# Scatter marks on one engine, attention products over the whole array, and six more steps before a transpose

## The chip, the core and the metric

The kernel runs on one core of one Trainium2 chip. The core has five engines with queues of their own: PE (TensorE, matrix products; its weight loads are listed as PEld), DVE (VectorE), ACT (ScalarE), POOL (GpSimd) and SP, which issues most transfers. Each queue runs in the order in which it was laid out; between queues, instructions wait on semaphores. The metric is the device time of one execution in microseconds.

## The reference

A network of three blocks on 512 tokens of width 1024, batch 1, all in float32:

```python
def reference(x, ...):
    x = first_block(x, ...)        # hybrid mixer (recurrence and pooling), then expert layer
    return second_block(x, ...)    # even mixer, conv FFN, odd mixer, conv FFN

def peer_ffn(h, wq, keys, u_tab, v_tab):             # the expert layer, 16384 experts
    q = (xb @ wq).reshape(T, 8, 2, 128)
    s = einsum('thpc,hpnc->thpn', q, keys)           # two key halves, 128 scores each
    v1, i1 = top_k(s[:, :, 0], 16); v2, i2 = top_k(s[:, :, 1], 16)
    sc, pos = top_k(v1[..., :, None] + v2[..., None, :], 16)   # over 256 candidates
    idx, gate = take_along_axis(i1 * 128 + i2, pos), softmax(sc)
    act = gelu(einsum('td,thkd->thk', xb, u_tab[idx]))
    return einsum('thk,thkd->td', gate * act, v_tab[idx])

# even mixer: MLA attention (8 heads, values of 64) and difference attention (4 heads, two maps of 64 rows)
# odd mixer: dilated attention (3 groups of 4 heads of 64, one joint softmax) and
#            stick-breaking attention (4 heads of 64); both causal, blocks of 128 queries
```

## The kernel before

A float32 weight tile of 1024 columns is loaded, rounded by ACT into a high part (L64) and split by DVE or POOL into a low part (L67); three products per pair (`mm3`, L117 to L119) replace one in full precision. `K.unit` does load, cast and split. Where no engine is named for the split, POOL and DVE take turns.

The program is traced by Python generators and then laid out: for each engine the planner orders the instructions by the moment at which its own model has them ready, with program order as priority, so the queues don't follow the program line by line. `interleave(main, n_main, fill, n_fill)` mixes two generators step by step: after step i of `main`, `fill` has made i * n_fill / n_main steps.

**Expert layer.** The first 128 tokens ("gathered" tokens) fetch their experts' rows one by one with indirect transfers of POOL (`chosen`, L621). For the other 384 tokens the layer is computed densely: for each of 128 expert tiles `up` makes 24 products of 384 columns (tile `pu`), the result is multiplied by a gate and `down` adds it into `pacc`. The gates come from `scatter` (L483): in 24 groups of 16 tokens, each with 4 steps of 4 tokens, one-hot marks are formed and multiplied: `gu` (L498, 128 elements per partition) and `lw` (L500, 256) mark the two parts of an index, `gu` is multiplied by the gate (L502), `e[1]` marks the other half (L507, 512 elements) and `e[0]` is the product of `gu` and `lw` (L511). `e[0]` is shared out: POOL makes four tokens' worth in the even steps and three in the odd ones, where DVE makes the fourth. PE multiplies `e[0]` by `e[1]` (L517), 8 instructions a step, ACT copies the gates out (L520, L521), and SP sends most of them to memory (`pe_gd`).

While search and scatter run, `ahead` computes the first `EARLY` expert tiles: `FIRST` steps after each of seven heads of the search, the rest interleaved with `scatter`. The dense stage then starts with `EARLY` tiles that need no `up`, two steps of `chosen` beside each, and goes on with 118 - `EARLY` tiles interleaved with the rest of `chosen` and then `end`. `end` (L725) squares the gathered tile on ACT, yields once, and then normalises, transposes on PE (`pf`) and evicts it.

**Attention.** `Attn.scores` makes one product per segment (`sp`, L785), `transposed` turns the probabilities (`tp`, L805), and the values follow (`po`). The products run in float32, each as two instructions of PE. MLA scores use 96 rows. MLA values (L999) take 64 columns of the array per head, two heads sharing a bank. Difference scores, dilated scores (tiles `od_qk`) and stick scores (L1114) use 64 rows of a tile that holds two heads; dilated values (L1191) and stick values (L1142) 64 columns. In the odd block, `proj` copies each projected tile out of PSUM on ACT, and `out` turns a finished pair of heads into a high and a low part. The projections that are still missing fill the steps of the attention.

Of the kernel before, what the change touches and what calls it, by code (L numbers as in the profile page):

```python
# [13 lines left out]
F32 = mybir.dt.float32  # L14
# [9 lines left out]
S = 512  # L24
# [310 lines left out]
EARLY = 25  # L335
# [64 lines left out]
class Peer:  # L400
# [84 lines left out]
    def scatter(self, wk, ps, slots, pool, iota):  # L485
# [6 lines left out]
        own = 0, 1, 0, 1  # L492
        for t16 in range(NB):
            ts = slice(16 * t16, 16 * t16 + 16)
            g = wk.tile([128, 16, 8], F32, name=k.name("gu"), tag="gu")
            lw = wk.tile([128, 16, 16], BF16, name=k.name("lw"), tag="lw")
# [5 lines left out]
            (V if t16 else G).tensor_tensor(out=g, in0=g, in1=slots[:, 0, ts].unsqueeze(2).to_broadcast([128, 16, 8]), op=ALU.mult)  # L502
            for q in range(4):
# [5 lines left out]
                for eng, lo, hi in ((G, 0, 4 - own[q]), (V, 4 - own[q], 4)):  # L509
                    if lo < hi:  # L510
                        eng.tensor_tensor(out=e[0][:, lo:hi].rearrange("p t (u l) -> p t u l", u=8),  # L511
                                          in0=g[:, 4 * q + lo:4 * q + hi].unsqueeze(3).to_broadcast([128, hi - lo, 8, 16]),
                                          in1=lw[:, 4 * q + lo:4 * q + hi].unsqueeze(2).to_broadcast([128, hi - lo, 8, 16]),
                                          op=ALU.mult)
# [130 lines left out]
    def run(self, x, free_x, dram, ctx2, pre, ps, tag):  # L645
# [9 lines left out]
        with ExitStack() as ctx, ExitStack() as gctx, ExitStack() as ectx:  # L655
# [57 lines left out]
            with open_pool(tc, name="pe_gc", bufs=2) as self.gpool:  # L713
                interleave(dense, 118 - EARLY, chained(fill, self.end(st, 0, acc, g, gpre, tail, ps)), 252)
# [10 lines left out]
    def end(self, st, t, u, g, gpre, pool, ps):  # L725
# [13 lines left out]
        yield  # L739
# [100 lines left out]
def finished(k, st, gen, gpost, gpre, pool):  # L840

    for done in gen:
# [7 lines left out]
        yield  # L850

# [5 lines left out]
def even(k, st, a, pre):  # L857
# [3 lines left out]
    with ExitStack() as ctx:  # L861
# [26 lines left out]
        with open_pool(tc, name="ev_lr", bufs=1) as lr, open_pool(tc, name="ev_wk", bufs=2) as wk:  # L888
# [96 lines left out]
            def mla(h, i):  # L985
# [10 lines left out]
                if j not in po:  # L996
                    po[j] = st.bank("po")
                for b in range(i + 1):
                    T.matmul(po[j][z * 64:z * 64 + 64, q], vm[:, b, h * 64:(h + 1) * 64], pT[b],  # L999
                             start=b == 0, stop=b == i)  # L1000
                if z == 1 and i == NT - 1:
                    p = po.pop(j)
                    A.copy(ohi[j], p)
                    V.tensor_tensor(out=olo[j], in0=p, in1=ohi[j], op=ALU.subtract)
# [14 lines left out]
        def diff(h, i):  # L1019
# [3 lines left out]
            for z in range(2):  # L1023
                rows = slice(64 * z, 64 * z + 64)
                ss.append(at.scores([(dq[h][rows, q], dk[h][rows, 0:n], n, 0.125, bias[:, h, 512 - n:])],
                                    512, "s" if z else "s2"))
# [27 lines left out]
def odd(k, st, a, pre):  # L1054
# [3 lines left out]
    with ExitStack() as ctx:  # L1058
# [7 lines left out]
        qk = [tile(f"od_qk{i}") for i in range(12)]  # L1066
# [24 lines left out]
        def out(j, p, q=slice(0, S)):  # L1091
            A.copy(ohi[j][:, q], p)
            V.tensor_tensor(out=olo[j][:, q], in0=p, in1=ohi[j][:, q], op=ALU.subtract)

        with open_pool(tc, name="od_st", bufs=2) as wk:
# [4 lines left out]
            sq = [wk.tile([128, S], F32, name=f"od_s{i}", bufs=1) for i in range(4)]  # L1100
            po = {}

            def stick(h):

                z, j = h % 2, h // 2
                rows = slice(64 * z, 64 * z + 64)
                q, kt = sq[j], sq[2 + j]
# [3 lines left out]
                for kb in (3, 2, 1, 0):  # L1111
                    n = 512 - 128 * kb
                    zp = st.bank("sp")
                    T.matmul(zp[:, :n], kt[rows, kb * 128:(kb + 1) * 128], q[rows, kb * 128:], start=True, stop=True)  # L1114
# [22 lines left out]
                if j not in po:  # L1137
                    po[j] = st.bank("po")
                p = po[j]
                for kb in range(4):  # L1140
                    n = 512 - 128 * kb
                    T.matmul(p[rows, kb * 128:], vt[:, kb, 768 + h * 64:768 + (h + 1) * 64],  # L1142
                             at_[:, off[kb]:off[kb] + n], start=kb == 0, stop=kb == 3)
                yield
                if z == 1:
                    out(j, po.pop(j))
# [989 lines left out]
```

## Time and profile before

| | us |
|---|---|
| three runs | 3182.52, 3187.62, 3186.67 (median 3186.67) |
| profiled execution | 3186.87, its span 3185.1 |
| busy in the span: PE, PEld | 3011.8 (95%), 2505.0 (79%) |
| busy: DVE, ACT, POOL | 2045.6 (64%), 1344.0 (42%), 1021.9 (32%) |
| chain that ended last | PE 68%, DVE 7%, the rest 1% and less each |

The stages in this execution: mixer to about 500 us, search of the expert layer to 699, scatter to 873, dense experts to 1858, even block to some 2115, FFN to some 2515, odd block to some 2820, FFN to the end. Busy shares are means over stages with different limits, so the table by stage is what to read first. PE's matmuls overlap: one instruction's duration holds its latency, and the distance from one start to the next is what it costs in a stream. The same is true, by some 0.08 us, of DVE.

### The profile page before, as it was taken

Reading aid. Unit: us, or ns where it says so; the run is one execution under the profiler, and the core shown is the slowest. Engines: PE = TensorE matmul, PEld = TensorE weight load, DVE = VectorE, ACT = ScalarE, POOL = GpSimd, SP = SyncE. Lnnn points to the kernel's source line nnn. Section 1 sums busy time; section 2 is a strip of 40 time slices with the busy share of each in tenths; the row PEclk is TensorE's granted clock in tenths of the full one; section 3 lists DMA queues with packets and bytes.
Section 4 is the critical chain, followed back from the end, with each engine's and each line's share of the span. In section 5 each row is a group of like instructions: output and inputs, shape, how many; then the busy total and the mean of one; then the engine's idle time right before and its main releaser. Section 6 shows DMA issues by size and latency. Waiting matters only on the chain.

```text
span 3185.1 us, 45861 instructions
## 1 busy us (share of the span) xinstructions
PE 3011.8 (95%) x17602; PEld 2505.0 (79%) x17602; DVE 2045.6 (64%) x3762; ACT 1344.0 (42%) x2448; POOL 1021.9 (32%) x754
## 2 busy tenths in 40 slices
PE   7888999998799999999999999989999999999999
PEld 5656668988678998999998986668888776688887
DVE  5777747999987888888888445565551333554522
ACT  5333344346633333333334355564442354444422
POOL 4322234667612444444443021222222221122221
PEclk9878999999999999999999999999999999999999
DMA  2000134333346999999998432323233242123332
GB/s 89 24 16 20 39 121 162 94 110 149 131 137 215 344 335 329 330 334 338 334 336 289 126 116 67 112 73 108 93 99 93 87 133 83 51 88 100 93 99 80
DMA packets 176203, 476.09 MB, mean 149 GB/s; under 512 B 18768, under 2 KB 68688, under 8 KB 175728
## 3 DMA queue, kind: packets, MB, share of 16 engines
q1 hardware_dynamic: 139120, 338.93, 32.2%
q0 software_dynamic: 36864, 134.23, 11.8%
q8 instruction: 138, 2.26, 0.3%
q14 instruction: 81, 0.66, 0.1%
HBM read 448.59 MB, written 24.51 MB: 149 GB/s over the span
## 4 chain that ended last, share of the span: by engine, by line
PE 68%; DVE 7%; issue 1%; ACT 1%; DMA 1%; POOL 0%; DVEq 0%; ACTq 0%; POOLq 0%
PE pacc L119 6%; PE pacc L117 5%; PE pacc L118 5%; PE up L117 5%; PE up L118 5%; PE up L119 5%; PE pu L117 5%; PE pu L119 5%; PE pu L118 5%; PE acc L117 3%; PE acc L119 3%; PE acc L118 3%; DVE e L507 2%; PE pj L117 2%; PE pj L118 2%; PE pj L119 2%
## 5 line engine op out<-in xcount | busy, mean ns | idle before, releaser
L64 ACT CAST whi<-raw 128x1024 fp32r<-128x1024 f32 x494 | 518.1, 1051 | 685.3 <-PE pu L118 173.8
L67 DVE TENSOR_TENSOR wlo<-raw,whi 128x1024 fp32r<-128x1024 f32 x359 | 454.5, 1267 | 446.6 <-ACT whi L64 444.6
L67 POOL TENSOR_TENSOR wlo<-raw,whi 128x1024 fp32r<-128x1024 f32 x135 | 328.7, 2436 | 1109.9 <-ACT whi L64 1040.7
L117 PE MATMUL pu<-pe_hhi,whi 128*128 128x384 f32 x1024 | 350.5, 342 | 6.2 <-ACT whi L64 3.7
L119 PE MATMUL pu<-pe_hhi,wlo 128*128 128x384 f32 x1024 | 348.6, 340 | 0.2 <-DVE wlo L67 0.2
L118 PE MATMUL pu<-pe_hlo,whi 128*128 128x384 f32 x1024 | 348.1, 340 | 0.0
L118 PE MATMUL pacc<-wlo,ahi 128*128 128x512 f32 x768 | 304.1, 396 | 0.0
L117 PE MATMUL pacc<-whi,ahi 128*128 128x512 f32 x768 | 296.2, 396 | 3.1 <-ACT ahi L592 3.1
L119 PE MATMUL pacc<-whi,alo 128*128 128x512 f32 x768 | 292.2, 398 | 3.4 <-DVE alo L593 3.4
L119 PE MATMUL up<-res_h,wlo 128*128 128x512 f32 (+1 forms) x752 | 283.2, 377 | 1.0 <-DVE wlo L67 1.0
L117 PE MATMUL up<-res_h,whi 128*128 128x512 f32 (+1 forms) x752 | 283.8, 378 | 0.0
L118 PE MATMUL up<-res_h,whi 128*128 128x512 f32 (+1 forms) x752 | 283.5, 377 | 0.0
L621 POOL DMA_INDIRECT row<-pe_v,pe_gs x128 | 160.4, 1253 | 217.6 <-DVE pe_acc L637 208.5
L621 POOL DMA_INDIRECT row<-pe_rows,pe_gs x128 | 163.9, 1281 | 185.5 <-DVE pe_gs L628 165.7
L253 DVE SCALAR_TENSOR_TENSOR u<-up,ffn_par,u 128x511 f32<-128x511 f32 (+1 forms) x176 | 131.4, 748 | 142.7 <-ACT u L251 139.6
L117 PEld LDWEIGHTS pu<-pe_hhi,whi 128*128 128x128 f32 x1024 | 193.9, 189 | 11.6 <-ACT whi L64 4.2
L118 PEld LDWEIGHTS pu<-pe_hlo,whi 128*128 128x128 f32 x1024 | 194.0, 189 | 4.3
L119 PEld LDWEIGHTS pu<-pe_hhi,wlo 128*128 128x128 f32 x1024 | 193.6, 189 | 1.1 <-DVE wlo L67 0.8
L119 PEld LDWEIGHTS pacc<-whi,alo 128*128 128x128 f32 x768 | 144.9, 189 | 38.2 <-DVE alo L593 3.8
L117 PEld LDWEIGHTS pacc<-whi,ahi 128*128 128x128 f32 x768 | 144.7, 189 | 33.2 <-ACT ahi L592 3.8
L118 PEld LDWEIGHTS pacc<-wlo,ahi 128*128 128x128 f32 x768 | 144.8, 188 | 31.0
L637 DVE SCALAR_TENSOR_TENSOR pe_acc<-row,pe_gs,pe_acc 128x1024 f32<-128x1024 f32 x128 | 163.7, 1279 | 5.9 <-DMA row<-pe_v,pe_gs 5.5
(499 smaller groups left out, 6557.3 us busy)
## 6 DMA issues: line engine op xcount, KB each, us to landing
raw<-pe_u SPq DMA_DIRECT2D x128, 512.0 KB, 5.9
raw<-pe_v SPq DMA_DIRECT2D x128, 512.0 KB, 6.1
raw<-ffn_up SPq DMA_DIRECT2D x88, 512.0 KB, 3.5
raw<-ffn_dn SPq DMA_DIRECT2D x44, 512.0 KB, 3.6
pe_gd<-go SPq DMA_DIRECT2D x24, 784.0 KB, 3.3
gc<-pe_gd SPq DMA_DIRECT2D x12, 1536.0 KB, 15.5
mraw<-mx_in SPq DMA_DIRECT2D x80, 128.0 KB, 2.2
raw<-pe_wq SPq DMA_DIRECT2D x16, 512.0 KB, 3.8
```

Source lines behind the costliest of these rows:

```text
L64: nc.scalar.copy(hi, raw)
L67: eng.tensor_tensor(out=lo, in0=raw, in1=hi, op=ALU.subtract)
L117: mm(out, l[0], r[0], start=first, stop=False)
L118: mm(out, l[0], r[1], start=False, stop=False)
L119: return mm(out, l[1], r[0], start=False, stop=last)
L253: V.scalar_tensor_tensor(out=u[:, d:], in0=p[:, :S - d], scalar=par[:, o + 2 - d:o + 3 - d], in1=u[:, d:], op0=ALU.mult, op1=ALU.add)
L507: V.tensor_tensor(out=e[1], in0=slots[:, 3, o:o + 4].unsqueeze(2).to_broadcast([128, 4, 128]), in1=iota.unsqueeze(1).to_broadcast([128, 4, ...
L621: G.indirect_dma_start(out=r, out_offset=None, in_=table[z], in_offset=bass.IndirectOffsetOnAxis(ap=idx[:, j:j + 1], axis=0))
L637: V.scalar_tensor_tensor(out=acc, in0=row("v", j), scalar=w[:, j:j + 1], in1=acc, op0=ALU.mult, op1=ALU.add)
```

## The change

It has three parts. In `scatter` all products `e[0]` and the first `gu` product go to DVE, `gu` and `lw` move from the pool `wk` to the pool of `go`, `EARLY` is 26 instead of 25, and the splits of the early expert tiles from number 11 on are all given to DVE. In the attention, MLA, dilated and stick products use 128 rows and columns: queries are kept once per head with zeros in the other head's 64 rows (`apart`, `blank`), values multiply the columns of both heads, and each head has a bank (or, for the last dilated heads, half of one) of which its own 64 rows are evicted. In `end`, the gathered tile yields seven times between squares and transposes, and the filler's count is 258 instead of 252.

```diff
-EARLY = 25
+EARLY = 26
@@ scatter
-        own = 0, 1, 0, 1
-            g = wk.tile([128, 16, 8], F32, name=k.name("gu"), tag="gu")
-            lw = wk.tile([128, 16, 16], BF16, name=k.name("lw"), tag="lw")
+            g = pool.tile([128, 16, 8], F32, name=k.name("gu"), tag="gu")
+            lw = pool.tile([128, 16, 16], BF16, name=k.name("lw"), tag="lw")
-            (V if t16 else G).tensor_tensor(out=g, in0=g, in1=slots[:, 0, ts]...)
+            V.tensor_tensor(out=g, in0=g, in1=slots[:, 0, ts]...)
-                for eng, lo, hi in ((G, 0, 4 - own[q]), (V, 4 - own[q], 4)):
-                    if lo < hi:
-                        eng.tensor_tensor(out=e[0][:, lo:hi]..., op=ALU.mult)
+                V.tensor_tensor(out=e[0].rearrange("p t (u l) -> p t u l", u=8),
+                                in0=g[:, 4 * q:4 * q + 4]..., in1=lw[:, 4 * q:4 * q + 4]..., op=ALU.mult)
@@ ahead
-            early.append((yield from self.up(pool, ps, hhi, hlo, i, f"early{i}")))
+            eng = self.k.nc.vector if UP * i >= 7 * FIRST else None
+            early.append((yield from self.up(pool, ps, hhi, hlo, i, f"early{i}", eng)))
@@ run
-                interleave(dense, 118 - EARLY, chained(fill, self.end(st, 0, acc, g, gpre, tail, ps)), 252)
+                interleave(dense, 118 - EARLY, chained(fill, self.end(st, 0, acc, g, gpre, tail, ps)), 258)
@@ end
-        yield
+        for _ in range(1 + 6 * (t == 0)):
+            yield
@@ new
+HALF = (slice(0, 64), slice(64, 128))
+def apart(k, dst, src):
+    k.nc.scalar.copy(dst[0][HALF[0]], src[HALF[0]])
+    k.nc.vector.tensor_copy(dst[1][HALF[1]], src[HALF[1]])
+def blank(k, pairs):
+    for z in range(2):
+        for pair in pairs:
+            k.nc.gpsimd.memset(pair[z][HALF[1 - z]], 0.0)
@@ mla
-                if j not in po:
-                    po[j] = st.bank("po")
+                if i == 0:
+                    po[h] = st.bank("po")
-                    T.matmul(po[j][z * 64:z * 64 + 64, q], vm[:, b, h * 64:(h + 1) * 64], pT[b], ...)
-                if z == 1 and i == NT - 1:
-                    p = po.pop(j)
-                    A.copy(ohi[j], p)
+                    T.matmul(po[h][:, q], vm[:, b, j * 128:(j + 1) * 128], pT[b], ...)
+                if i == NT - 1:
+                    p = po.pop(h)[HALF[z]]
+                    A.copy(ohi[j][HALF[z]], p)
@@ odd
-        qk = [tile(f"od_qk{i}") for i in range(12)]
+        pool = (fctx.enter_context(open_pool(tc, name="od_j0", bufs=1, side="right")), big)
+        qs = [[tile(f"od_q{i}{z}", pool=pool[i % 2]) for z in range(2)] for i in range(6)]
+        ks = [tile(f"od_k{i}", pool=pool[i % 2]) for i in range(6)]
+        blank(k, qs)
-                A.copy(qk[f], st.project1(k.unit(a["od_in"][f]), "pj"))
+                p = st.project1(k.unit(a["od_in"][f]), "pj")
+                if f < 6:
+                    apart(k, qs[f], p)
+                else:
+                    A.copy(ks[f - 6], p)
-        def out(j, p, q=slice(0, S)):
+        def out(h, p, q=slice(0, S)):
+            j, r = h // 2, HALF[h % 2]
+            A.copy(ohi[j][r, q], p[r])
-            sq = [wk.tile([128, S], F32, name=f"od_s{i}", bufs=1) for i in range(4)]
+            sq, sk = (qs[1], qs[3]), (ks[1], ks[3])
@@ stick
-                    T.matmul(zp[:, :n], kt[rows, kb * 128:(kb + 1) * 128], q[rows, kb * 128:], ...)
+                    T.matmul(zp[:, :n], kt[:, kb * 128:(kb + 1) * 128], q[:, kb * 128:], ...)
-                    T.matmul(p[rows, kb * 128:], vt[:, kb, 768 + h * 64:768 + (h + 1) * 64], ...)
+                    T.matmul(p[:, kb * 128:], vt[:, kb, 768 + j * 128:896 + j * 128], ...)
@@ dilated
-                segs.append((qk[f][rows, q], qk[6 + f][rows, lo * 128:n], w, 0.125, ...))
+                segs.append((qs[f][z][:, q], ks[f][:, lo * 128:n], w, 0.125, ...))
-            p = po[key][rows, 0:128] if j else po[key][rows, q]
+            p = po[key][:, z * 128:z * 128 + 128] if j else po[key][:, q]
-                T.matmul(p, vt[:, kb, hd * 64:(hd + 1) * 64], pT[b], ...)
+                T.matmul(p, vt[:, kb, f * 128:(f + 1) * 128], pT[b], ...)
+        fctx.close()
```

## Rows read from the trace of the kernel before

**Rows 1.** Busy us by stretch: PE, PEld, DVE, ACT, POOL (instructions), clock, DMA share, GB/s.
```profile
500.00:699.00 199.00, 185.62 (x1349) 182.70 (x1348) 178.84 (x709) 79.01 (x164) 117.16 (x78) 0.99 0.34 110
699.00:873.00 174.00, 138.12 (x947) 127.28 (x945) 168.31 (x221) 113.42 (x401) 120.33 (x100) 0.96 0.35 134
1030.00:1858.00 828.00, 826.40 (x4113) 746.92 (x4113) 637.73 (x789) 301.29 (x420) 319.53 (x256) 1.00 0.87 305
1938.00:2046.00 108.00, 105.11 (x537) 76.60 (x536) 52.09 (x133) 55.11 (x122) 19.33 (x8) 1.00 0.26 83
2556.00:2685.00 129.00, 129.00 (x535) 92.88 (x534) 49.69 (x94) 66.85 (x122) 29.66 (x13) 1.00 0.36 112
2685.00:2800.00 115.00, 113.99 (x594) 78.16 (x593) 55.14 (x174) 51.13 (x101) 12.50 (x8) 1.00 0.16 49
```

**Rows 2.** Timeline of DVE in the scatter stage, POOL silent until 737.76: start, us, instruction.
```profile
736.64 0.41 DVE L500 TENSOR_TENSOR lw<-pe_slots,pe_iota 128x256 bf16<-128x256 f32 x1
736.98 0.68 DVE L507 TENSOR_TENSOR e<-pe_slots,pe_iota 128x512 f32<-128x512 f32 x1
737.58 0.28 DVE L511 TENSOR_TENSOR e<-gu,lw 128x128 f32<-128x128 f32 x1
737.78 0.28 DVE L502 TENSOR_TENSOR gu<-gu,pe_slots 128x128 f32<-128x128 f32 x1
```

**Rows 3.** Timeline of POOL and DVE in the scatter stage, later.
```profile
840.68 1.13 POOL L511 TENSOR_TENSOR e<-gu,lw 128x512 f32<-128x512 f32 x1 [0.53 <-PE gp L517]
840.83 1.27 DVE L500 TENSOR_TENSOR lw<-pe_slots,pe_iota 128x256 bf16<-128x256 f32 x1
842.62 0.92 DVE L511 TENSOR_TENSOR e<-gu,lw 128x128 f32<-128x128 f32 x1
```

**Rows 4.** Timeline of PE around one score product, in MLA and the odd block.
```profile
1950.86 0.39 PE L119 MATMUL pj<-res_h,wlo 128*128 128x512 f32 x1
1951.09 0.60 PE L785 MATMUL sp<-kh,qh 96*128 96x256 f32 x2
1951.76 0.40 PE L118 MATMUL pj<-res_h,whi 128*128 128x512 f32 x1
...
2692.14 0.40 PE L119 MATMUL pj<-res_h,wlo 128*128 128x512 f32 x1
2692.47 0.70 PE L785 MATMUL sp<-od_qk,od_qk 64*128 64x256 f32 x2
2693.43 0.40 PE L118 MATMUL pj<-res_h,whi 128*128 128x512 f32 x1
```

**Rows 5.** Source view of L67 (ns min/median/max), DVE waits, groups by line.
```profile
L67 DVE TENSOR_TENSOR wlo<-raw,whi x5: 1207/1212/1225, 711.6 to 775.4; 128x1024 fp32r<-128x1024 f32 x5
...
L67 POOLq EVENT_SEMAPHORE  x13: 17/43/4923, 601.1 to 690.6; - x13
...
DVE wlo L67 <- ACT whi L64: 1.9, 1, 1.9
...
L1799 POOL MEMSET TT<- 128x1024 f32 x4 | 3.8, 952 | 7.7 <-PE rp L1817 7.7
```

**Rows 6.** Timeline of PE in the scatter stage.
```profile
731.09 0.34 PE L117 MATMUL pu<-pe_hhi,whi 128*128 128x384 f32 x1
731.27 0.33 PE L118 MATMUL pu<-pe_hlo,whi 128*128 128x384 f32 x1
731.79 2.84 PE L517 MATMUL gp<-e,e 128*128 128x128 f32 x24
```

**Rows 7.** Instructions by line, with first and last start: MLA values, dilated scores.
```profile
L999 PE MATMUL po<-pT,ev_vm x160: 272/273/324, 1939.7 to 2044.1; 128*64 128x128 f32 x160
...
L785 PE MATMUL sp<-od_qk,od_qk x96: 272/480/693, 2675.6 to 2780.0; 64*128 64x256 f32 x40, 64*128 64x128 f32 x24, 64*128 64x384 f32 x16, 64*128 64x512 f32 x16
```

**Rows 8.** Timeline of PE in the stick part.
```profile
2578.70 0.92 PE L1114 MATMUL sp<-od_s,od_s 64*128 64x384 f32 x4
2579.55 0.50 PE L117 MATMUL pj<-whi,res_h 128*128 128x512 f32 x1
```

More of the change, by code (lines that the diff above doesn't have):

```diff
@@ L1023, in diff @@
             for z in range(2):
-                rows = slice(64 * z, 64 * z + 64)
-                ss.append(at.scores([(dq[h][rows, q], dk[h][rows, 0:n], n, 0.125, bias[:, h, 512 - n:])],
+                ss.append(at.scores([(dq[h][HALF[z], q], dk[h][HALF[z], 0:n], n, 0.125, bias[:, h, 512 - n:])],
                                     512, "s" if z else "s2"))
@@ L1105, in stick @@
                 z, j = h % 2, h // 2
-                rows = slice(64 * z, 64 * z + 64)
-                q, kt = sq[j], sq[2 + j]
+                q, kt = sq[j][z], sk[j]
                 lk = wk.tile([128, 1280], F32, name=k.name("lk"), tag="lk")
@@ L1113, in stick @@
                     zp = st.bank("sp")
-                    T.matmul(zp[:, :n], kt[rows, kb * 128:(kb + 1) * 128], q[rows, kb * 128:], start=True, stop=True)
+                    T.matmul(zp[:, :n], kt[:, kb * 128:(kb + 1) * 128], q[:, kb * 128:], start=True, stop=True)
                     t = wk.tile([128, 512], F32, name=k.name("sz"), tag="sz")
@@ L1136, in stick @@
                     yield
-                if j not in po:
-                    po[j] = st.bank("po")
-                p = po[j]
+                p = st.bank("po")
                 for kb in range(4):
                     n = 512 - 128 * kb
-                    T.matmul(p[rows, kb * 128:], vt[:, kb, 768 + h * 64:768 + (h + 1) * 64],
+                    T.matmul(p[:, kb * 128:], vt[:, kb, 768 + j * 128:896 + j * 128],
                              at_[:, off[kb]:off[kb] + n], start=kb == 0, stop=kb == 3)
                 yield
-                if z == 1:
-                    out(j, po.pop(j))
-            for y, p in zip((sq[0], sq[2], sq[1]), st.project([k.unit(a["od_in"][f]) for f in (12, 14, 13)], "lr")):
-                A.copy(y, p)
-            A.copy(sq[3], st.project1(k.unit(a["od_in"][15]), "pj"))
+                out(h, p)
+            for y, p in zip((sq[0], sk[0], sq[1]), st.project([k.unit(a["od_in"][f]) for f in (12, 14, 13)], "lr")):
+                apart(k, y, p) if isinstance(y, list) else A.copy(y, p)
+            A.copy(sk[1], st.project1(k.unit(a["od_in"][15]), "pj"))
             run_all(values(1))
@@ L1171, in dilated @@
             z, j = hs % 2, hs // 2
-            rows = slice(64 * z, 64 * z + 64)
             segs, vals = [], []
@@ L1177, in dilated @@
                 w = n - lo * 128
-                segs.append((qk[f][rows, q], qk[6 + f][rows, lo * 128:n], w, 0.125,
+                segs.append((qs[f][z][:, q], ks[f][:, lo * 128:n], w, 0.125,
                              bias[g][:, z, (512 if g else 256) - w:]))
-                vals += [(4 * g + hs, kb) for kb in range(lo, i + 1)]
+                vals += [(f, kb) for kb in range(lo, i + 1)]
             s, sm = at.scores(segs, 1280, "s")
@@ L1185, in dilated @@
             pT = at.transposed(s, len(vals))
-            key = (j, i) if j else j
+            key = (j, i) if j else hs
             if key not in po:
                 po[key] = st.bank("po")
-            p = po[key][rows, 0:128] if j else po[key][rows, q]
-            for b, (hd, kb) in enumerate(vals):
-                T.matmul(p, vt[:, kb, hd * 64:(hd + 1) * 64], pT[b], start=b == 0, stop=b == len(vals) - 1)
-            if z == 1 and (j or i == NT - 1):
-                p = po.pop(key)
-                if j:
-                    out(3, p[:, 0:128], q)
-                else:
-                    out(2, p)
+            p = po[key][:, z * 128:z * 128 + 128] if j else po[key][:, q]
+            for b, (f, kb) in enumerate(vals):
+                T.matmul(p, vt[:, kb, f * 128:(f + 1) * 128], pT[b], start=b == 0, stop=b == len(vals) - 1)
+            if j:
+                out(4 + hs, p, q)
+            elif i == NT - 1:
+                out(4 + hs, po[key])
+            if (z or not j) and (j or i == NT - 1):
+                po.pop(key)
         load_bias(0)
```

17 lines of the change are left out of this document (7 added, 10 removed).

## The prediction

> **What bounds the kernel now.** I first read the busy time by stage [rows 1] and looked in each stage for the engine with no air left. In the dense expert stage (1030 to 1858 us) that is PE: 826.4 of 828 us busy at a granted clock of 1.00. In the MLA attention (1938 to 2046) and in the odd block's attention (2556 to 2800) it is PE too: 105.1 of 108 us, 129.0 of 129, 114.0 of 115, while DVE and ACT stay at or under 52%. Only in the scatter stage (699 to 873) it is another engine: DVE 168.3 of 174 us, PE 138.1. So only what frees DVE in the scatter stage, or PE time elsewhere, is worth anything.
>
> Then I asked what DVE does in the scatter stage. With POOL silent, one mark of 512 elements starts 0.60 us before the next instruction, the 256-element one (L500) 0.34 us, a 128-element one 0.20 us [rows 2]. With POOL inside its own product (L511) the same instructions stretch: L500 lasts 1.27 us against 0.41, and ends 0.29 us after POOL's does; the 128-element L511 lasts 0.92 against 0.28 [rows 2, 3]. The reader is to see that DVE isn't working there but is held until POOL is through. Last, in the attention I compared two PE excursions of equal size. A score product over 96 rows, between full-array projection products, stretches the way from the first projection product to the third to 0.90 us; one over 64 rows, with the same 256 columns, to 1.29 us [rows 4]. The difference, 0.39 us, is two changes of array shape.
>
> **The change part by part.** The sum is made against the profiled execution: 3186.87 us, of which the span is 3185.1 and 1.8 lie around it; the median of the runs shown is 3186.67, so both are one time.
>
> *Scatter marks.* Removed: 96 POOL products. Added to DVE: the same products whole, 512 elements instead of 128 in every second one. A 512-element product is priced like L507, 0.60 us from start to start, since 0.20, 0.34 and 0.60 us for 128, 256 and 512 elements lie on one line whichever line of the program it is [rows 2]. Per 16 tokens: 0.20 + 0.34 + 0.20 + 4 x (0.60 + 0.60) = 5.54 us; 24 such groups make 133 us. Now these lines fill the stage's 174 us but for five splits of weight tiles (5 x 1.14 = 5.7 us by their spacing; 1.21 each [rows 5]). Splits come on top: `ahead` now puts those of expert tiles 11 to 25 all on DVE, where before they alternated with POOL. That is 15 instead of 7, and 8 x 1.14 = 9 us more, some of it in the search stage, whose DVE is busy 178.8 of 199 us [rows 1]; I count it as lost in either. So 174 - (168 - 133) + 9 = 148, a gain of 26, and one more from the 5.7 us in which DVE idles there [rows 1]: **-27**. Is PE then late next? 768 mark products at 0.11 us [rows 6] are 86 us; 947 instructions in the stage less 768 are 7.5 expert tiles of 24 products [rows 1], at 0.17 us each [rows 6] 4.1 us a tile, 31 us. Together 117, with one tile more 121: under 148. Bounds: nothing hidden elsewhere goes wrong, -36; if the search stage pulls no tile ahead any more, all 15.5 tiles fall into the scatter stage, PE needs 86 + 64 = 150 us plus its waits, and -12 is left.
>
> *The 26th early tile.* One expert tile (24 products, 4.1 us) moves from the PE-bound dense stage under the DVE-bound scatter stage, where PE idles 36 us [rows 1]: **-4**. It goes to 0 if that cover is gone. Its buffer comes from the two tiles that leave `wk`; these now wait for the memory of the search, which the marks wait for anyway: 0.
>
> *Six steps, and 258 for 252.* The transposes of the gathered tile come six steps of the filler later while the gather goes 258/92 = 2.80 steps per dense step instead of 252/93 = 2.71. PE is busy for 826.4 of 828 us there, so at most 1.6 us can be won [rows 1], and what is moved only trades places in a full queue: 0. On SP nothing of these steps is queued; the gathers on POOL come 3.5% faster. The cost would be traffic: DMA is busy 0.87 on the stage's mean at 305 GB/s [rows 1], with the gather in its first part. Bounds -1.6 to +7 (a dense step of 8 us stretched by 1% over 85 steps).
>
> *Whole array in the attention.* MLA values, dilated scores and values, stick scores and values now use 128 rows and 128 columns; half of the product is zeros or unread. A product's time goes by its moving columns, which stay, so nothing is added as long as two halves do not run abreast. Removed are the shape changes. On PE's timeline I count 56 between MLA values and their neighbours, and 134 in the odd block from 2556 to 2800 ([rows 7]: first and last start of the MLA values and of the dilated scores). Half of 0.39 us is 0.19; I take 0.18, as waits hide some ends: 190 x 0.18 = 34 us of PE time. Diff scores keep their 64 rows. Against it: some pairs of halves do run abreast. A score product is two instructions, and each streams its columns twice: two over 256 columns cost 0.90 - 2 x 0.23 = 0.44 us net [rows 4], which is 2 x 2 x 256 columns at 2.4 GHz. Four instructions over 384 columns take 0.85 us up to the next projection [rows 8], where one after the other they need 1.28 us and the shape change. I find two clear pairs in the stick part and one or two in the dilated part, 1.5 us lost. Of the 32.5 left I take 28, since in the last 85 us the filler thins out and DVE (55 of 115 us) with its chain score, exponent, transpose is next: **-28**, bounds -36 and -10.
>
> Here the Trainium skill speaks against the change: TensorEngine Tiling (Array Packing), section Key Properties, says that tiles operate independently and that different tiles can load and multiply in parallel. By that rule two half products cost as one and padding them doubles them. This trace shows it for the pairs above and not as the habit; what the rule would give is the second rival.
>
> *What padding adds elsewhere.* Twelve POOL memsets of 512 elements: 0.95 us for 1024 [rows 5], so about 0.5 each, 6 us, near the feed that opens the odd block; POOL's power operations for that feed queue with them, and the splits. Eight evictions become one on ACT and one on DVE; eleven more output copies go to each. At 0.68 us [rows 2] for 19 it is 13 us on DVE over 400 us of attention: hidden by PE at 52% or less. I take **+2** for memsets in the way; bounds 0 and +13, the latter if that cover were gone.
>
> Sum: 3186.87 - 27 - 4 - 28 + 2 = 3129.9, say **3130 us**.
>
> **The rivals.**
> 1. *Next bound comes early.* PE's waits in the scatter stage (its share of the pulled-ahead tiles) leave 15 of the 27 us, and attention's latency half of the 28: 3130 + 12 + 14 = 3156. For it: PE already shows 138 of 174 us. Against: PE waits there for DVE alone.
> 2. *Halves ran abreast.* By the sizes in the code the odd block's scores and its values have 18.9k columns each, MLA's values 10.2k; streamed four times at 2.4 GHz that is 31.6, 31.6 and 17.1 us. If all had run in pairs, padding would add half, 40 us, to the 34 removed: attention goes from -28 to +6, 3164. Against: the lone products of rows 4 are the common sight ([rows 8] the rare one). The skill's page named above is the rule behind this one.
> 3. *Traffic.* The faster gather holds up expert tiles in the dense stage: +7, 3137.
> 4. *Slower: splits block DVE.* DVE's queue is in order. A split waits for ACT's cast, and behind it stand search steps and marks that PE needs. On POOL a split waited up to 4.9 us in the search stage [rows 5]. If all 15 splits waited so on DVE: 15 x 4.92 = 74 us, 3204. It decides from 63 / 15 = 4.2 us a split on. Against: DVE's splits wait 1.9 us in all in the scatter stage [rows 5], and an order made for readiness moves with them.
> 5. *No contention.* If the long marks were the operands' own doing, the whole product would cost DVE as much as L500 at its longest, some 1.2 us [rows 3], 96 x 0.6 = 57 us more: 3187, no change. Against: the short ones [rows 2] have the same operands.
>
> **How the numbers follow.** Forecast 59%, rivals 17, 6, 8, 6 and 4% in this order. The forecast's own bounds are -27 - 4 - 28 taken at their best ends, 3108, and with one of the large terms at its worse end, 3148. The range 3108 to 3172 takes in rivals 1 to 3 with a few us of noise; outside are rivals 4 and 5 and some 9% beyond either end. A measurement of this kernel can tell 0.2% (6.4 us) from no change: below 3180 lie the forecast and rivals 1 to 3 but for their tails, 88%; around 3187 rival 5 and a piece of 4, 5%; above 3193 the rest, 7%.
>
> **What would show it.** Scatter stage: POOL silent, L507 and L511 each some 0.68 us long in every row, 16 tokens in about 5.6 us, the stage some 148 us. A mark at 1 us or more without POOL beside it breaks this step. Attention: no 0.10 us gaps around score products, MLA and odd stages shorter by 9 and 19 us; equal length with PE showing waits for ACT or DVE would be rival 1, longer score stretches rival 2. Dense: one tile less, 4 us; PE waiting for casts there would be rival 3. Above 3180 the first large term must have failed.

## The result and the profile after

The changed kernel takes 3150.43 us, median of 4 runs (3145.17 to 3154.2), against 3184.6 for the kernel before (3178.31 to 3187.62): ratio 0.9892, 95% interval 0.9879 to 0.9904, or 34 us less. The forecast was 3130, 57 us less; the measured time lies in the forecast's range (3108 to 3172), 20 us above the forecast itself. The profiled execution is the slowest of the four, 3154.2 us, with a span of 3152.4, which is 32.7 less than the span before, and it is on this pair of spans that the ledger is made.

The ledger cuts a trace at events that every version has: the last `pt` of the search, the last mark product `gp`, the first and last `pacc` of the dense stage, the last value product of MLA, the last of the difference attention, the end of the even block's output, ACT's first and last reading of a stick score, the last dilated value product, PE's last product. The row "even output to first stick score" starts at the last value product of the difference attention. 9.7 us of the span, the same in both executions, stand in no row: they lie between the last mark product and the first `pacc`, and behind PE's last product. Lengths in us:

| | before | after | change | forecast |
|---|---|---|---|---|
| mixer, not touched, to the first `pq` | 500.1 | 502.0 | +1.9 | 0 |
| search | 196.2 | 197.2 | +1.0 | in the scatter's -27 |
| scatter | 175.5 | 156.7 | **-18.8** | -27 |
| dense | 989.1 | 990.0 | **+0.9** | -4 |
| MLA | 181.4 | 175.0 | -6.4 | -9 |
| difference attention | 79.9 | 84.9 | **+5.0** | 0 |
| even output to first stick score | 432.8 | 436.0 | +3.2 | +2 |
| stick, dilated | 240.4 | 221.9 | -18.5 | -19 |
| the rest | 380.0 | 379.0 | -1.0 | 0 |

So three rows are to be explained: the scatter stage, short by 8 us, the dense stage, which gives its tile back, and the difference attention, which nobody touched.

First the stages of the changed kernel, in the columns of [rows 1]; the second and third row are the scatter stage, whose first 50 us differ from the rest.

```profile
699.00:750.00 51.00, 51.00 (x353) 51.00 (x351) 42.80 (x77) 32.59 (x97) 0.00 (x0) 1.00 0.45 157
750.00:857.00 107.00, 83.50 (x621) 74.28 (x620) 103.43 (x202) 82.47 (x306) 0.00 (x0) 1.00 0.37 149
1030.00:1700.00 670.00, 670.00 (x3342) 605.46 (x3341) 549.84 (x685) 237.72 (x327) 309.75 (x239) 1.00 0.94 336
1700.00:1720.00 20.00, 13.73 (x65) 11.57 (x63) 16.97 (x17) 6.38 (x11) 4.63 (x4) 0.90 0.78 270
1720.00:1740.00 20.00, 15.46 (x75) 14.96 (x76) 6.86 (x10) 7.40 (x13) 1.56 (x5) 0.76 0.09 28
1925.00:2024.00 99.00, 97.28 (x532) 80.27 (x531) 55.38 (x137) 56.92 (x126) 19.50 (x8) 0.98 0.28 91
2543.00:2645.00 102.00, 102.00 (x445) 80.36 (x444) 45.28 (x89) 60.18 (x112) 26.08 (x12) 1.00 0.35 114
2645.00:2766.00 121.00, 118.67 (x675) 97.25 (x674) 64.18 (x190) 60.95 (x119) 16.04 (x10) 1.00 0.21 70
```

In the scatter stage POOL is silent and DVE's busy time is 42.8 + 103.4 = 146.2 us, close to the forecast length of the stage. But in the first 51 us PE has no air at all while DVE idles 8.2; only behind them is DVE the bound (103.4 of 107). In the dense stage PE, full until 1700, loses 10.8 us in the next 40, and its clock falls: the same 20 us stretches were 20.00 busy at 1.00 before.

The marks and their products by line in the scatter stage:

```profile
L506 DVE TENSOR_TENSOR e<-pe_slots,pe_iota 128x512 f32<-128x512 f32 x96 | 64.5, 680 | 5.3 <-PE gp L513 5.3
L508 DVE TENSOR_TENSOR e<-gu,lw 128x512 f32<-128x512 f32 x96 | 64.5, 680 | 0.0
L513 PE MATMUL gp<-e,e 128*128 128x128 f32 x768 | 101.2, 280 | 22.6 <-DVE e L508 18.2 <-ACT go L517 2.2
```

DVE's waits there (waiter, releaser, us in all, times, longest):

```profile
DVE e L506 <- PE gp L513: 5.3, 3, 2.4
DVE wlo L67 <- ACT whi L64: 4.8, 4, 1.3
DVE gl L587 <- ACT gm L516: 1.6, 1, 1.6
```

These are nearly all of the 11.8 us that DVE idles in the 158 us of the two stretches: 5.3 us it waits for PE itself, 4.8 for casts of ACT. Those casts in turn wait for PE's expert products (ACT's waits in the same window):

```profile
ACT whi L64 <- PE pu L118: 13.2, 7, 2.8
```

All 192 marks last 0.68 us on the mean, those of L508 no longer than those of L506; their starts are 0.60 us apart, as in [rows 2] and never as in [rows 3]. (L506, L508 and L513 are before's L507, L511 and L517.)

The dense stage's hole, on PE's timeline, and below it the same transposes before the change:

```profile
1712.17 1.56 PE L119 MATMUL pacc<-whi,alo 128*128 128x512 f32 x6
1724.00 1.97 PE L190 MATMUL pf<-ident,xn 128*128 128x128 f32 x8 [10.26 <-DVE xn L185]
```

```profile
1749.16 1.03 PE L190 MATMUL pf<-ident,xn 128*128 128x128 f32 x8
```

PE stands for 10.26 us before the transposes `pf` of the gathered tile. Counted from the last mark product, PE is at this place of its queue after 857.9 us; before, it began them after 877.4 us (at 1749.2) and waited for nothing. The gathered tile itself isn't late: ACT squares it 862.8 us after the last mark product, 867.3 before. The place in PE's queue can be counted: before, the `up` products of 115 of the 128 expert tiles (2760 instructions) start ahead of the first `pf`, after, those of 114 (2736). A tile takes PE 8.4 us there; the tile that went to the scatter stage and a wait of 3.7 us that is gone (below) are most of the rest of the 19.5 us.

Score products in MLA and in the dilated part, the counterpart of [rows 4]:

```profile
1936.24 0.39 PE L119 MATMUL pj<-res_h,wlo 128*128 128x512 f32 x1
1936.47 0.60 PE L783 MATMUL sp<-kh,qh 96*128 96x256 f32 x2
1936.72 0.59 PE L117 MATMUL pj<-res_h,whi 128*128 128x512 f32 x1
1937.14 0.40 PE L118 MATMUL pj<-res_h,whi 128*128 128x512 f32 x1
...
2676.39 0.39 PE L119 MATMUL pj<-res_h,wlo 128*128 128x512 f32 x1
2676.61 0.59 PE L783 MATMUL sp<-od_k,od_q 128*128 128x256 f32 x2
2676.86 0.59 PE L117 MATMUL pj<-res_h,whi 128*128 128x512 f32 x1
2677.28 0.59 PE L783 MATMUL sp<-od_k,od_q 128*128 128x256 f32 x2
```

From the projection product ahead of the score to the instruction behind the next projection product it takes 1937.14 - 1936.24 = 0.90 us around MLA's 96 rows, as before, and 2677.28 - 2676.39 = 0.89 us around the dilated score, where 64 rows took 1.29 [rows 4].

### The profile page after: what moved, and what is told of

The parts are those of the page before. It is cut to its first block, busy times and chain, and to the rows that moved or that the text cites. A ratio compares the mean times of both kernels' runs of the same rounds, so it can differ in the third digit from the quotient of the medians.

```text
span 3152.4 us, 45760 instructions
## 1 busy us (share of the span) xinstructions
PE 2982.1 (95%) x17602; PEld 2514.9 (80%) x17602; DVE 2030.4 (64%) x3837; ACT 1348.7 (43%) x2459; POOL 906.1 (29%) x662
## 5 line engine op out<-in xcount | busy, mean ns | idle before, releaser
L67 DVE TENSOR_TENSOR wlo<-raw,whi 128x1024 fp32r<-128x1024 f32 x366 | 457.4, 1250 | 459.5 <-ACT whi L64 457.5
L67 POOL TENSOR_TENSOR wlo<-raw,whi 128x1024 fp32r<-128x1024 f32 x128 | 310.5, 2427 | 1085.6 <-ACT whi L64 994.3
```

Of the source, the lines that this page charges most:

```text
L67: eng.tensor_tensor(out=lo, in0=raw, in1=hi, op=ALU.subtract)
```

## The experiments

Ten kernels, and second profiles of the kernels before and after. The parts of the change are first taken apart, then the causes. The ledger of the ones that carry the verdicts, in us by the same events (the mixer's end, in code that no version touches, lies between 493 and 503). A row is one profiled execution, a median that of four to six executions, and a ratio is to the kernel before, timed beside that version:

| | search | scatter | dense | MLA | diff. | to stick | stick, dil. | median | ratio to before, 95% |
|---|---|---|---|---|---|---|---|---|---|
| before | 196.2 | 175.5 | 989.1 | 181.4 | 79.9 | 432.8 | 240.4 | 3184.6 | |
| after | 197.2 | 156.7 | 990.0 | 175.0 | 84.9 | 436.0 | 221.9 | 3150.43 | 0.9879 to 0.9904 |
| attn_alone | 196.2 | 173.1 | 985.8 | 174.6 | 77.5 | 436.1 | 221.3 | 3161.34 | 0.9919 to 0.9946 |
| scatter_alone | 198.1 | 156.7 | 988.9 | 182.1 | 82.2 | 433.7 | 240.4 | 3174.99 | 0.9958 to 0.9982 |
| filler_252 | 196.5 | 156.4 | 978.5 | 173.7 | 83.6 | 436.1 | 221.7 | 3139.97 | 0.9843 to 0.9873 |
| one_step | 197.3 | 156.4 | 1001.6 | 174.5 | 87.6 | 436.2 | 221.7 | 3163.98 | 0.992 to 0.9947 |
| marks_shared | 199.6 | 171.1 | 989.1 | 173.7 | 77.5 | 436.0 | 221.8 | 3158.43 | 0.9891 to 0.9927 |
| splits_alternating | 196.2 | 155.8 | 990.4 | 173.7 | 83.1 | 436.8 | 221.5 | 3145.72 | 0.9846 to 0.9885 |
| marks_one_pass | 197.2 | 149.2 | 987.8 | 174.7 | 83.1 | 436.1 | 221.7 | 3143.82 | 0.985 to 0.9886 |

How far such a row repeats: the second profile of the kernel before differs from the first by 0.3 us at most in any of these stages; that of the changed kernel by 3.9 us in the difference attention, 1.6 in the dense stage, 1.1 in the search and 0.6 or less elsewhere.

**The attention part alone, on the kernel before** (the diff is the attention's part of the change).

> The kernel before with the attention part alone. Theory: the attention is worth the 26 us that the two traces show at its values and scores (MLA 8, stick 5, dilated 13), and the 5 us that the difference attention gives back (its products run longer at the 1.2 GHz level) and the 3 us at the start of the odd block (memsets on POOL ahead of a power operation) belong to this part: 26 - 8 = 18 us faster than before, about 3167. Rival: the two losses come from the other parts of the change, which shift the clock's phases: 26 us faster, about 3159.

Measured: 23 us faster. MLA, stick and dilated are shorter by 6.8 + 5.1 + 14.0 = 25.9 us, and the start of the odd block is 3.3 longer: that loss belongs to this part. The 5 us of the difference attention don't: it is 2.4 us shorter here. So the theory is right on the start of the odd block, the rival on the difference attention. The profiled execution is the fastest of the five (3155.35 us), and stages that this part doesn't touch are shorter in it too (scatter 2.4 us, dense 3.3), for a reason that isn't known.

**The scatter part alone, on the kernel before** (marks, pools, `EARLY`, splits; one yield and 252).

> The kernel before with the scatter part alone: marks, their pool, 26 early tiles, splits of the later early tiles on DVE; one yield and a filler count of 252 as before. Theory: the scatter stage is worth 18 us, not 27, since PE is the bound of its first 50 us; and the dense stage loses its one tile's 4 us again, because with 92 instead of 93 dense steps the filler goes faster and the gathered tile's transposes stand in PE's queue ahead of the gather's end, with a stall of some 10 to 13 us: about 14 us faster than before, 3171. Rival: the stall belongs to the six steps and the 258: no stall here, 18 + 4 + 4 = 26 us faster, about 3159.

Measured: 10 us faster by the medians, 14 by the stages from the search to the difference attention (+1.9 - 18.8 - 0.2 + 0.7 + 2.3). By the medians the two parts add up to the whole: 23.5 + 9.8 = 33.3 of 34.2 us. The stall is there without the six steps and without the 258:

```profile
PE pf L190 <- DVE xn L185: 10.3, 1, 10.3
```

So the rival falls: this part's one edit of the dense stage, a tile less with the count left at 252, already puts the transposes too early (behind 114 tiles, as in the changed kernel), and the six steps and the 258 together change nothing in it.

**The filler's count.**

```diff
-... self.end(st, 0, acc, g, gpre, tail, ps)), 258)
+... self.end(st, 0, acc, g, gpre, tail, ps)), 252)
```

> The changed kernel with the filler count back at 252 and the six steps kept. Theory: the stall of 10.3 us before the gathered tile's transposes comes from their place in PE's queue; at 252 steps for 92 dense steps they come some 215/2.739 - 215/2.804 = 1.8 dense steps, 15 us, later, after the gather's real end: the stall is gone, and the time of lower clock behind it too, 10 to 14 us faster than the changed kernel, about 3138. Rival: the gather itself is late and slower pacing moves its end as much: no difference, 3150.

Measured: 10.5 us faster than the changed kernel, all of it in the dense stage (978.5 instead of 990.0). PE doesn't wait for `pf` at all there, and the clock is 0.91 or more in the two 20 us stretches from 1700 on. ACT squares the gathered tile 862.6 us after the last mark product, nearly the same as with 258, and the last row of the gather lands after 858.0 us instead of 859.0: the gather is hardly moved by the pace of its steps. The transposes are: they stand behind 116 tiles, and PE gets there after 873.7 us instead of 857.9.

**The steps.**

```diff
-        for _ in range(1 + 6 * (t == 0)):
-            yield
+        yield
```

> The changed kernel with one step instead of seven between squares and transposes of the gathered tile; 258 kept. Theory: the transposes then stand 6/2.80 = 2.1 dense steps, 17 us, earlier in PE's queue while the gather ends when it did: the stall grows from 10.3 to 27 us, about 3167. Rival, as the prediction had it: the steps only trade places in a full queue: no difference, 3150.

Measured: 13.5 us slower; the wait grows from 10.3 to 22.0 us (PE's waits), and the clock falls to 0.57 after it (the stretches). The wait is 5 us shorter than expected. The transposes stand behind 112 tiles and PE gets there 16.7 us earlier, after 841.1 us, but the gather ends a little earlier too: its last row lands after 856.3 us, and ACT squares the tile after 857.7. Why it does isn't shown.

```profile
PE pf L190 <- DVE xn L185: 22.0, 1, 22.0
```

```profile
1690.00:1710.00 20.00, 7.77 (x34) 5.88 (x32) 15.29 (x14) 3.66 (x4) 9.57 (x8) 0.75 0.91 313
1710.00:1730.00 20.00, 9.71 (x39) 9.31 (x40) 7.26 (x10) 6.03 (x13) 1.56 (x5) 0.57 0.07 28
```

The two runs settle it: two tiles' place of these transposes in PE's queue is worth 11.5 us of the dense stage in either direction.

**The marks given back to POOL.** In the changed kernel, `e[0]` is again shared out between POOL and DVE, and the first `gu` product goes to POOL.

```diff
-                V.tensor_tensor(out=e[0]..., op=ALU.mult)
+                for eng, lo, hi in ((G, 0, 4 - own[q]), (V, 4 - own[q], 4)):
+                    if lo < hi:
+                        eng.tensor_tensor(out=e[0][:, lo:hi]..., op=ALU.mult)
```

> The changed kernel with the marks shared between POOL and DVE as before (also the first gate product on POOL); their pool, 26 early tiles, DVE's splits, the attention and the steps stay. Theory (POOL inside its own product holds DVE's marks): the scatter stage, from the end of the search's last transposes to the last mark product, goes back from 156.7 us to before's 175.5 and some 4 to 8 us more, since four to seven more splits lie on DVE: 180 to 183, the whole 3150 + 25 = 3175. Rival (the marks cost DVE the same wherever their other half is made, and the gain is that of the early tiles and the pool): the stage keeps under 160 us, 3152.

Measured: scatter 171.1, so 14.4 longer: in the direction of the theory, and less than it expected. The search, in which no mark runs, is 2.4 longer. The span of the profiled execution is only 6.8 longer, since its difference attention is 7.4 us shorter; the medians differ by 8, and why by no more isn't shown. 4.4 of the 18.8 us stay although the marks are shared; they aren't taken apart. By line, over the scatter stage:

```profile
L507 DVE TENSOR_TENSOR e<-pe_slots,pe_iota 128x512 f32<-128x512 f32 x96 | 93.0, 989 | 1.5 <-PE gp L517 1.5
L511 DVE TENSOR_TENSOR e<-gu,lw 128x128 f32<-128x128 f32 x48 | 27.1, 564 | 0.0
L500 DVE TENSOR_TENSOR lw<-pe_slots,pe_iota 128x256 bf16<-128x256 f32 x24 | 23.2, 968 | 0.0
```

The unchanged mark L507 lasts 989 ns on the mean instead of 680 with POOL at work, the small ones twice as long as in [rows 2]: that is the contention. One place of the two timelines shows its form:

```profile
799.75 0.69 DVE L507 TENSOR_TENSOR e<-pe_slots,pe_iota 128x512 f32<-128x512 f32 x1 [0.33 <-PE gp L517]
800.35 1.15 DVE L498 TENSOR_TENSOR gu<-pe_slots,pe_iota 128x128 f32<-128x128 f32 x1
799.85 1.50 POOL L511 TENSOR_TENSOR e<-gu,lw 128x512 f32<-128x512 f32 x1 [2.79 <-PE gp L517]
```

The mark that began ahead of POOL's product keeps its 0.69 us; the small one behind it ends 0.15 us after POOL's product does. The Trainium skill (SBUF — State Buffer, section "SBUF: two separate sides") describes a port pair that DVE and GpSimd share under an exclusive lock. These rows agree with it; the mean of 989 ns alone would not tell a lock from a shared rate.

**The splits in turn again.**

```diff
-            eng = self.k.nc.vector if UP * i >= 7 * FIRST else None
-            early.append((yield from self.up(pool, ps, hhi, hlo, i, f"early{i}", eng)))
+            early.append((yield from self.up(pool, ps, hhi, hlo, i, f"early{i}")))
```

> The changed kernel with the splits of the later early tiles shared between POOL and DVE in turn, as before. Theory (contention): of the ten splits that DVE makes in the scatter stage, about five go to POOL, 5 x 1.14 = 5.7 us less work on DVE, but each holds DVE's marks; a product of 512 elements on POOL stretched one mark by 0.86 us [rows 2, 3], so one of 1024 costs about 1.7: 5 x 1.7 - 5.7 = 3 us longer, scatter 160 instead of 156.7, the whole 3153. Rival (the splits load DVE and POOL is free): scatter 151, the whole 3144.

Measured: scatter 155.8, search 196.2, 2 us less in all. Neither. Seven splits go back to POOL, four in the search and three in the scatter stage, these by 731, while PE is the bound and DVE has slack; so this run doesn't weigh contention against load. It shows that the place of the splits is worth some 2 us net, and that the 9 us that the sum counted for them are not there.

**Less work for PE in the scatter stage.**

```diff
-                e = [wk.tile([128, 512], F32, name=k.name("e"), ...
+                e = [wk.tile([128, 512], F32R, name=k.name("e"), ...
```

> The changed kernel with the mark tiles in the rounded format of the expert tiles, so that PE makes each mark product as one instruction in one pass instead of two that stream twice; this changes part of the computation: the gates are rounded to that format. DVE's work is the same. Theory (the scatter stage's bound alternates: PE, full of mark products and nine early tiles, for its first 50 us, DVE after it, and DVE idles some 11 us in all beside PE): the stage falls from 156.7 to 145 to 149 us, the whole to about 3141. Rival (DVE bounds the stage all through, as the prediction's sum had it, and its marks are simply slower than the sum had them): no difference, 156 to 157, 3150.

Measured: scatter 149.2, 7.5 us less, with as many marks on DVE, 0.60 us apart as before (each lasts 0.72 us instead of 0.68): the theory's upper end, and nothing of the rival. The stage in two stretches:

```profile
699.00:750.00 51.00, 47.35 (x306) 46.86 (x305) 47.94 (x84) 36.45 (x111) 0.00 (x0) 0.98 0.51 181
750.00:852.00 102.00, 76.16 (x293) 67.21 (x294) 100.47 (x199) 78.79 (x295) 0.00 (x0) 0.50 0.36 148
```

And DVE's waits for PE and for ACT's casts, 5.3 and 4.8 us in the changed kernel, then those of the casts, 13.2 there:

```profile
DVE e L506 <- PE gp L513: 2.6, 3, 1.6
DVE wlo L67 <- ACT whi L64: 0.4, 1, 0.4
ACT whi L64 <- PE pu L118: 3.5, 2, 2.7
```

DVE now works 47.9 of the first 51 us instead of 42.8, and the rest is DVE-bound as before (100.47 of 102): PE's clock is 0.50 there, and the stage still gets no longer.

**The memsets.** Two tries. In the first, with 252, `blank` is called right ahead of each `apart`.

```diff
-        blank(k, qs)
+                if f < 6:
+                    blank(k, [qs[f]])
                     apart(k, qs[f], p)
```

> The changed kernel with the filler count at 252 and the twelve memsets put right ahead of the copies into their tiles instead of at the opening of the odd block. Theory (six memsets, 2.95 us of POOL in one row, hold the power operation of the feed that opens the odd block): from the end of the even block's output to the first stick score 415 us become 412, the whole 3140 - 3 = 3137. Rival (the 3 us come from the two halves' copies and the order, not from the memsets): 415, 3140.

Measured: 3136.6 us (0.9826 to 0.986), but the stretch in question stays at 435.9 us (the expectation's 415 is the same stretch counted from the end of the even output, 21 us later), since the planner puts six memsets where they were, in a row of 3.32 us on POOL at 2478.57. The edit did nothing to the suspect; where its trace is shorter than that of 252 alone, it is so in the dense stage (3.0 us) and the difference attention (4.0). On the memsets it is inconclusive. In the second, ACT writes the zeros:

```diff
-        blank(k, qs)
@@ apart
+    for z in range(2):
+        k.nc.scalar.activation(dst[z][HALF[1 - z]], src[HALF[1 - z]], AF.Copy, scale=0.0)
```

> The changed kernel with the filler count at 252 and without the memsets: ACT writes the zeros when a projected query tile is copied, from the same tile with scale 0. Theory (the six memsets in a row hold POOL's power operation for the feed): from the end of the even block's output to the first stick score 415 us become 412 to 413, the two more ACT copies ahead of it costing up to 1, the whole some 2 us under the 3140 of the kernel with 252 alone. Rival (the 3 us come from the halves' copies and the order of the queue): 415 to 416, no gain.

Measured: 3137.49 us (0.9827 to 0.9858). The feed that opens the odd block, in the changed kernel (POOL, then PE) and here:

```profile
2502.00 2.95 POOL L864 MEMSET od_q<- 64x512 f32 x6
2504.92 0.53 POOL L177 TENSOR_TENSOR ms<-ms,mhalf 128x1 f32<-128x1 f32 x1
...
2510.97 1.94 PE L190 MATMUL feed<-ident,xn 128*128 128x128 f32 x8 [10.03 <-DVE xn L185]
```

```profile
2493.89 1.97 PE L190 MATMUL feed<-ident,xn 128*128 128x128 f32 x8 [7.62 <-DVE res_h L193]
```

Without the memsets PE waits 7.62 us, as it did before the change (7.60), instead of 10.03: 2.4 us is their price in this wait. The first stick score comes 10 us earlier rather than 3, but stick and dilated together are 8 us longer (229.8), since the order of the projections around them has changed; 1.8 us remain over the three stretches, no more than executions of one program differ by, and the median is not below that of the first try, which kept the memsets. In the whole time their price isn't shown.

**The best found.** The same with one-pass marks.

> The same, and the mark tiles in the rounded format, so that PE makes a mark product in one pass (the gates are rounded to that format). Theory: the scatter stage's 7.5 us add up with the dense stage's 10 and the memsets' 2: some 3130. Rival (a scatter stage that ends earlier lets the gather's transposes wait again, as the gather goes by its transfers): 3134 to 3138, with a wait of some us before the gathered tile's transposes.

Measured: 3129.51 us (0.9806 to 0.9841), scatter 149.2, dense 980.2, no wait before `pf`: the gains add up. It is faster than both kernels, with gates that are rounded; the fastest with the gates as they were are the two in which the memsets were tried, at 3137.

**The same programs again**, for the difference attention.

> The kernel before, for a second profile of the same program. Theory (the length of the difference attention follows the granted clock of the single execution, not the change): its 79.9 us and its mean clock of 0.89 will not be met again exactly, but some pair on the same line, from 77.5 at 0.96 to 87.6 at 0.81. Rival (each program has its own value): 79.9 at 0.89 again.

> The changed kernel, for a second profile of the same program. Theory: as for the second profile of before, a difference attention between 77.5 and 87.6 us that goes with its mean granted clock. Rival (the change itself slows it): 84.9 us at 0.82 again.

The difference attention alone, as a window from the last value product of MLA to its own last (columns as in [rows 1]). Before:

```profile
2044.10:2124.00 79.90, 70.31 (x301) 45.58 (x299) 58.35 (x184) 51.38 (x136) 13.19 (x8) 0.89 0.17 53
```

Before, again:

```profile
2045.60:2125.50 79.90, 70.34 (x301) 45.59 (x299) 58.37 (x184) 51.41 (x136) 13.23 (x8) 0.89 0.17 53
```

The changed kernel:

```profile
2022.70:2107.60 84.90, 76.01 (x300) 49.26 (x300) 58.74 (x184) 51.72 (x136) 12.61 (x8) 0.82 0.16 50
```

The changed kernel, again:

```profile
2025.40:2106.30 80.90, 71.98 (x300) 46.14 (x299) 58.49 (x184) 51.54 (x136) 12.63 (x8) 0.87 0.17 53
```

The attention alone:

```profile
2031.50:2109.00 77.50, 66.90 (x301) 43.54 (x299) 58.06 (x184) 51.69 (x136) 12.63 (x8) 0.96 0.17 55
```

The marks shared:

```profile
2037.00:2114.50 77.50, 66.91 (x300) 43.67 (x300) 58.04 (x184) 51.69 (x136) 12.61 (x8) 0.96 0.17 55
```

One step:

```profile
2034.50:2122.10 87.60, 77.46 (x300) 49.13 (x299) 58.61 (x184) 51.46 (x136) 13.18 (x8) 0.81 0.15 49
```

The instructions are the same, DVE's and ACT's busy time too; the length follows the clock, 77.5 us at 0.96 to 87.6 at 0.81. The changed program gave 84.9 in one execution and 80.9 in the next, so the +5 isn't work that the change adds, and 4 of it come and go with the program as it is. Whether the change moves the mean isn't settled: the four executions with shared marks lie between 77.5 and 79.9 us, the ten with the marks on DVE between 77.5 and 87.6. My expectation that before would not repeat its own value missed: it did, to a tenth. What decides how long PE stays at the 1.2 GHz level here isn't settled by these runs.

## Why the prediction was right or wrong

The time lies in the range because the two large terms came with the right mechanism, one almost whole and one at two thirds. The number is nearer to rival 1's 3156 than to the forecast's 3130, but only the scatter half of that rival happened. (By the terms' own bounds the lower end of the range adds up to 3109, not 3108.)

1. **Scatter marks, -27: mechanism right, size off by 8.** The marks cost 0.68 us in every row, POOL is silent, and sharing them out again costs 14.4 us in this stage: contention was there and is gone. DVE is busy for 146.2 us, close to the 148 that the sum gave the whole stage. The step that failed is "Is PE then late next?", answered with one sum for the whole stage (121 us under 148). PE's work isn't spread evenly: all the early tiles that are left, eight and a quarter, run in the first 53 us, where PE is full and DVE idles. The sum gave DVE no idle time; it idles 11.8 us over the stage, 5.3 behind PE's mark products and 4.8 behind casts that wait for PE. Taking PE work away made the stage 7.5 us shorter, and both waits fell. It is rival 1's first half (15 of the 27 left), with 18.8 left. The bound of -12 was reached by counting the same PE work, but again as one sum.

2. **The splits' 9 us within that term: wrong.** Put back in turn they change search and scatter by 2 us. Nine lie in the scatter stage, all by 755, most of them in PE's stretch, where DVE has time. Rival 4, in which a split waits 4.2 us and more on DVE, falls: DVE waits 4.8 us for casts in the whole stage. Rival 5 falls by the 0.68 us.

3. **The 26th tile, -4, and the six steps, 0: the step that failed most plainly.** The sum said that what is moved "only trades places in a full queue". A queue that runs in order is full only as long as its next instruction is ready, and these transposes wait for a gather whose last row lands at nearly the same time (858.0, 859.0 and 856.3 us after the last mark product) wherever they stand (PE gets there after 873.7, 857.9 and 841.1). Steps of the filler decide at which dense tile they stand: the missing tile, with neither the six steps nor the 258 (scatter_alone), moves them forward enough to stall, and 252 instead of 258 moves them back. What was there to be had is shown by filler_252, 10.6 us shorter than before in this stage. The tile's 4 us are in it, and a wait of PE for a cast, before 1030, that is 3.5 to 3.8 us long in the three traces with 25 early tiles and 0.5 or less in those with 26; the rest isn't taken apart. In the changed kernel a stall of 10.3 us and a lower clock behind it took all of that. That the -4 ended near its own bound of 0 is by another way than the one named there, the lost cover under the scatter stage. The bound of "+7" for these steps was priced as traffic, rival 3, of which nothing is seen: PE is 670.00 of 670 us busy from 1030 to 1700 in both.

4. **Attention, -28: right.** 24.9 us in this trace, 25.9 with the part alone; the 3 us that are missing are MLA's (6.4 of 9). Padding a half product to the whole array shows no cost of its own (0.89 us around the padded score product, 0.90 around the one over 96 rows), and no engine took PE's place as the bound (102.0 of 102 and 118.7 of 121 us in the odd block). With 190 shape changes and the 1.5 us of lost pairs, a change is worth (24.9 + 1.5) / 190 = 0.14 us instead of the 0.18 that the sum took. Rival 2, that halves run abreast and padding ends at +6, falls. The rule behind it is in the Trainium skill (TensorEngine Tiling (Array Packing), Key Properties): tiles work in parallel; the same list says that a change of tiling mode drains the engine. In this kernel the second sentence fits the time and the first doesn't decide it, because most half products stand singly between full-array ones. The runs show time lost at the changes; that it is a drain they don't show.

5. **Padding elsewhere, +2: right in size.** The start of the odd block is 3.2 us longer, and 2.4 of it is PE's longer wait behind the memsets and POOL's power operation, as named. This rests on one wait in one execution; the whole time doesn't resolve it.

6. **Not in the sum: the clock.** The difference attention's +5 in the profiled execution goes with a lower granted clock, not with more work. Without it and the mixer's 1.9 the change in span is -39.6, and of the 57 us forecast the 17 that are missing are the scatter's 8, the search's 1, the dense stage's 5 and the attention's 3.

## What to carry to other kernels

Before a term is taken from an engine's idle time in a stage, cut the stage where the other engine's work lies: two engines can each be the bound in turn, and the sum over the stage hides it. Changing the number of main steps or the filler's count moves every instruction that is placed by step; look for those that wait for a transfer, whose end doesn't move with them, and place them behind it. A stage that is as long again at another granted clock, with the same instructions, is to be taken out of the comparison first.

## What the runs showed of the hardware

With one-pass marks PE had less to do in the scatter stage (76.2 us busy in 102), and its granted clock was 0.50 for all of the second stretch, where it was 1.00 with two passes (83.5 in 107). The gain of 7.5 us came although every product there ran at the 1.2 GHz level: an engine that isn't the bound can lose its clock at next to no cost (DVE was busy for 100.47 of the 102 us), and in both kernels with one-pass marks the clock fell where PE had less to do.
